# Moving the matmul operands of a decoder layer within their partitions, by padding

## The chip, the cores and the metric

The kernel runs on one core of a Trainium2 chip. The metric is the time of one execution on the device in microseconds, the median of several runs. One execution was also recorded by the hardware profiler; the rows below are from that one.

## What is computed

One layer of a decoder, for 512 tokens of 1024 features, all in float32. Cut to what matters here:

```python
def reference(x, p, ...):
    h = x
    h = h + 0.5 * rms_norm(swiglu(rms_norm(h, ffn1_pre_g), w_gate, w_up, w_down), ffn1_post_g)
    u = rms_norm(h, mix_pre_g)
    proj = u @ w_in                       # queries, keys, forget gates, merge gates, ...
    y_a = dsa_branch(...)                 # attention over keys that an indexer selects
    y_b = ...                             # gated linear recurrence, normed and gated
    merged = sigmoid(gate_a + b) * (y_a @ w_br_a) + sigmoid(gate_b + b) * (y_b @ w_br_b)
    h = h + rms_norm(merged @ w_out, mix_post_g)
    h = h + 0.5 * rms_norm(swiglu(rms_norm(h, ffn2_pre_g), w_gate, w_up, w_down), ffn2_post_g)
    ple_gate = sigmoid(rms_norm(h, ple_pre_g) @ w_ple_gate)
    return h + rms_norm(ple_gate * (p @ w_ple_proj), ple_post_g)

def swiglu(x, w_gate, w_up, w_down):
    return (silu(x @ w_gate) * (x @ w_up)) @ w_down       # 1024 -> 2816 -> 1024
```

## The kernel before

Activations lie with features on the 128 partitions and the 512 tokens along a partition. Every large product is made in three float32r matmuls: both operands are split into a high part, rounded to float32r, and a low part, the rest; the product is high x high, low weights x high, high weights x low, all added up in one bank of PSUM. `mm3_step` (line 205; all matmuls of this kind go through `matmul`, line 239) makes these three for one block of 128 input features: `w[:, 0]` is the high and `w[:, 1]` the low part of the weights, `hi` and `lo` those of the activations. A tile of weights is 128 x 1024, so one output block of 128 features takes 8 x 3 = 24 matmuls (21 where seven blocks are summed).

The weights are the stationary operand and the activations the moving one, 512 columns at a time, or 256 where a stage works on half of the tokens so that the norm behind it can start early. Each matmul has a weight load of its own. In a few products the two change places: for keys, values and the last gate the activations (`hg_hi`, `hg_lo`) are stationary and the weights moving.

Three pairs of tiles hold activations that feed products:

- `hg_hi`, `hg_lo` (made in `consts`, 8 x 512 elements of 4 bytes in each partition): the norm operands. They hold the scaled input of both feed-forward stages, of the mixers' projections and of the last gate, and for a while the two branches' outputs before they are merged.
- `hid_hi`, `hid_lo` (made in `ffn`, for each feed-forward stage): the hidden activations, operands of the second product, in three groups of 8, 7 and 7 blocks.
- `m_hi`, `m_lo` (made in `merge`): the merged mixers, operands of the product with `w_out`.

A weight comes from memory in one transfer (`raw`, three buffers), ScalarE writes its high part, VectorE or GpSimd its low part, into one of six tiles `w` of 2 x 1024 elements. Tiles are laid one behind the other in a partition in the order in which pools hand them out, so the size of an early tile moves all that follow. `r` (4 elements) and `R` (512) are the inverse norms of the tokens. The mixers' stage runs the projections beside the attention, its indexer and the recurrence in an order written out in a table (`PLAN`). The indexer's products have `kidxT` moving and `st` stationary (`dots`, line 508), the recurrence has float32 products of a tile `hX` with itself (lines 698 to 748).

Where these tiles begin in a partition, in bytes, in the program before: `hg_hi` 18336, `hg_lo` 34720, the six `w` 65440 and then every 8192, `hid_hi` and `m_hi` 164512, `hid_lo` and `m_lo` 180896. All of these are 160 modulo 256, and each block of 128 weights (512 bytes) and of 512 tokens (2048 bytes) begins at a multiple of 256 from its tile's start. `kidxT` is at 160 modulo 256 too; `st` is at 32.

Of the kernel before, what the change touches and what calls it, by code (L numbers as in the profile page):

```python
# [7 lines left out]
F32 = mybir.dt.float32  # L8
F32R = mybir.dt.float32r
# [5 lines left out]
P = 128  # L15
D = 1024
NT = 512
KT = D // P
# [52 lines left out]
class Layer:  # L71
# [27 lines left out]
    def consts(self):  # L99
        nc, c = self.nc, self.const  # L100
        self.ident = c.tile([P, P], F32, name="ident")
        self.vecs = c.tile([P, NVEC], F32, name="vecs")
        nc.sync.dma_start(self.vecs, self.a["vecs"])
        self.ones = c.tile([P, P], F32, name="ones")
        nc.gpsimd.memset(self.ones, 1.0)
        self.mhalf = c.tile([P, 16], F32, name="mhalf")
        nc.gpsimd.memset(self.mhalf, -0.5)
        self.ghalf = {}
        for n in ("ffn1_post", "ffn2_post"):
            t = c.tile([P, KT], F32, name=f"half_{n}")  # L110
            nc.vector.tensor_scalar_mul(t, self.gain(n), 0.5)
            self.ghalf[n] = t
        lb = self.vecs[:, LB:LB + 8].rearrange("p (l h) -> p l h", l=2)
        top = c.tile([P, HG], F32, name="lb_top")
        nc.vector.tensor_tensor(top, lb[:, 0], lb[:, 1], op=OP.max)
        e = c.tile([P, 2, HG], F32, name="lb_e")
        for l in range(2):
            nc.vector.tensor_tensor(e[:, l], lb[:, l], top, op=OP.subtract)
        nc.scalar.activation(e, e, AF.Exp)
        den = c.tile([P, HG], F32, name="lb_den")  # L120
        nc.vector.tensor_tensor(den, e[:, 0], e[:, 1], op=OP.add)
        nc.vector.reciprocal(den, den)
        self.lb = c.tile([P, HG], F32, name="lb")
        nc.vector.tensor_tensor(self.lb, e[:, 0], den, op=OP.mult)
        self.lb1 = c.tile([P, HG], F32, name="lb1")
        nc.vector.tensor_scalar(self.lb1, self.lb, -1.0, 1.0, op0=OP.mult, op1=OP.add)
        self.lbn = c.tile([P, HG], F32, name="lbn")
        nc.vector.tensor_scalar_add(self.lbn, self.lb, -1.0)

        self.r = self.keep.tile([P, 4], F32, name="r")  # L130
        self.hg_hi = self.keep.tile([P, KT, NT], F32R, name="hg_hi")
        self.hg_lo = self.keep.tile([P, KT, NT], F32R, name="hg_lo")
        self.R = self.keep.tile([P, NT], F32, name="R")

    def bias_vector(self):

# [235 lines left out]
    def ffn(self, name, nxt, y, pool, spill=None, begin=None):  # L372
        nc, a = self.nc, self.a
        wg, wu, wd = (a[f"{name}_w_{s}"] for s in ("gate", "up", "down"))
        post = self.ghalf[f"{name}_post"]
        hid_hi = pool.tile([P, 8, NT], F32R, name="hid_hi")
        hid_lo = pool.tile([P, 8, NT], F32R, name="hid_lo")
        acc = self.accum(NT)
        for f0, nf in GROUPS:
            first, last = f0 == 0, f0 + nf == FT  # L380
            j0 = 0
            if first and not begin:
                j0 = 2
                w = [self.first_weights(name, (wg[j], wu[j]), D) for j in range(j0)]
                for cols, tags in zip(HALF, (("mm", "mm", "pl", "pl"), ("pt", "po", "mm", "mm"))):
                    ps = [[self.bank(t)[:, :256] for t in tags[2 * j:2 * j + 2]] for j in range(j0)]
                    self.mm3s([(ps[j][i], w[j][i]) for j in range(j0) for i in range(2)], self.hg_hi, self.hg_lo, KT, cols)
                    for j in range(j0):
                        self.hidden(hid_hi, hid_lo, j, *ps[j], cols)
            elif first:  # L390
                j0 = 1
                w = begin[0](wg[0], wu[0])
                ps = self.bank("pl"), self.bank("pt")
                self.mm3s(list(zip(ps, w)), self.hg_hi, self.hg_lo, KT, FULL)
                begin[1]()
                self.hidden(hid_hi, hid_lo, 0, *ps, FULL)
            for j in range(j0, nf):
                pg, pu = self.bank(), self.bank()
                self.mm3(pg, self.weight(wg[f0 + j], D), self.hg_hi, self.hg_lo, KT, FULL)
                self.mm3(pu, self.weight(wu[f0 + j], D), self.hg_hi, self.hg_lo, KT, FULL)  # L400
                self.hidden(hid_hi, hid_lo, j, pg, pu, FULL)
            w = {}

            def product(m, cols):
                if m not in w:
                    w[m] = self.weight(wd[m][:, f0 * P:(f0 + nf) * P], nf * P)
                n = cols.stop - cols.start
                ps = self.bank()[:, :n]
                self.mm3(ps, w[m], hid_hi, hid_lo, nf, cols)
                if first:  # L410
                    nc.scalar.copy(y[:, m, cols], ps)
                else:
                    nc.vector.tensor_tensor(y[:, m, cols], y[:, m, cols], ps, op=OP.add)
                if last:
                    self.square_sum(acc[:, cols], y[:, m, cols], m == 0, nc.vector if m == KT - 1 else nc.gpsimd)

            if last:
                self.last_product(product, y, acc, post, nxt, TURN[name], spill)
                if begin:
                    self.ple_proj(pool)  # L420
            elif first and begin:
                for m in range(KT):
                    product(m, FULL)
                begin[2]()
            else:
                for m in range(KT):
                    product(m, FULL)
# [453 lines left out]
    def merge(self, pool):  # L881

        nc, a = self.nc, self.a
        y = pool.tile([P, KT, NT], F32, name="y_mix")
        m_hi = pool.tile([P, KT, NT], F32R, name="m_hi")
        m_lo = pool.tile([P, KT, NT], F32R, name="m_lo")
        w, first = {}, {}

        def branch(m, b):
            t = pool.tile([P, NT], F32, tag=f"g{b}", name=f"g{b}", bufs=LEAD + 2 if b == 0 else 2)  # L890
            j = b * KT + m
            nc.sync.dma_start(t, self.gate_d[j])
            nc.vector.tensor_tensor(t, t, self.R, op=OP.mult)
            nc.scalar.activation(t, t, AF.Sigmoid, bias=self.vecs[:, GATE_B + j:GATE_B + j + 1])
            if b == 0:
                w[m] = self.weight(a["w_br"][m], D)
            ps = self.bank()
            self.mm3(ps, w[m], self.hg_hi[:, 4 * b:4 * b + 4, :], self.hg_lo[:, 4 * b:4 * b + 4, :], 4, FULL, b * 512)
            nc.vector.tensor_tensor(t, t, ps, op=OP.mult)
            return t  # L900


        for i in range(KT + LEAD):
            if i < KT:
                first[i] = branch(i, 0)
            m = i - LEAD
            if m >= 0:
                t = branch(m, 1)
                nc.gpsimd.tensor_tensor(t, t, first[m], op=OP.add)
                self.split(m_hi[:, m, :], m_lo[:, m, :], t)  # L910
        for k in range(KT):
            nc.sync.dma_start(self.h[:, k, :], self.h_d[k])
        acc = self.accum(NT)
        w = {}

        def product(m, cols):
            if m not in w:
                w[m] = self.weight(a["w_out"][m], D)
            n = cols.stop - cols.start
            ps = self.bank()[:, :n]  # L920
            self.mm3(ps, w[m], m_hi, m_lo, KT, cols)
            nc.scalar.copy(y[:, m, cols], ps)
            self.square_sum(acc[:, cols], ps, m == 0, nc.vector if m == KT - 1 else nc.gpsimd)

        self.last_product(product, y, acc, self.gain("mix_post"), "ffn2_pre", TURN["mix"])
# [175 lines left out]
```

## Time and profile before

| | |
|---|---|
| median of three runs | 1253.28 us (1251.13 to 1253.41) |
| the profiled execution | 1254.52 us |
| its span, first to last instruction | 1252.7 us |
| TensorE busy | 1228.4 us, 6263 matmuls |
| VectorE busy | 706.7 us |
| ScalarE busy | 530.3 us |
| GpSimd busy | 297.8 us |
| moved from and to memory | 131.29 MB, mean 105 GB/s |

The profile's page gives the busy time of each engine over the span, and then groups of instructions by the line that issued them. A name like `mm<-hg_hi,w` says that a matmul wrote a PSUM tile of the tag mm and read hg_hi and w. The five tags mm, pl, pt, po and hg are the kinds of PSUM banks; a product goes to whichever is next in a ring. Matmuls are pipelined: one lasts longer than the distance to the start of the next, so the busy time of a group counts overlapping matmuls once, and the mean duration behind it is that of one.

### The profile page before, as it was taken

The numbers are of one execution on the slowest core, as the hardware profiler recorded it, in microseconds if no ns is written. First come the engines' busy times: TensorE is split into PE (matmuls) and PEld (weight loads), VectorE is DVE, ScalarE is ACT, GpSimd is POOL, SyncE is SP. The second block draws the span as 40 slices with busy tenths as digits, with TensorE's granted clock in tenths as the row PEclk, the third lists the DMA queues.
The fourth block names the chain that finished last, engine by engine and source line by source line (L and its number), as shares of the span: only waits on it lengthen the run. The fifth ranks groups of instructions, "written<-read, shape, count | busy, mean of one in ns | idle before, by whom it ended". The sixth has DMA issues, their size and how long they took to land.

```text
span 1252.7 us, 16616 instructions
## 1 busy us (share of the span) xinstructions
PE 1228.4 (98%) x6263; PEld 1031.5 (82%) x6263; DVE 706.7 (56%) x1252; ACT 530.3 (42%) x905; POOL 297.8 (24%) x348
## 2 busy tenths in 40 slices
PE   7999999999999999999999999999999999999997
PEld 5888888888898887888888877888888888888986
DVE  7543226444448659997677558295532444444386
ACT  6423213222336455565767554364332222222363
POOL 3000000000045203636857622360000000000374
PEclk9999999999999999999999999999999999999999
DMA  6433354333245402423221245223333333332141
GB/s 222 135 91 96 88 107 132 111 101 93 78 130 176 140 18 85 128 91 123 68 72 65 97 138 199 76 85 101 112 91 101 99 86 102 101 95 90 52 152 68
DMA packets 45576, 131.29 MB, mean 105 GB/s; under 512 B 5144, under 2 KB 10424, under 8 KB 45496
## 3 DMA queue, kind: packets, MB, share of 16 engines
q1 hardware_dynamic: 45496, 130.24, 33.3%
q8 instruction: 49, 0.80, 0.3%
q14 instruction: 31, 0.25, 0.1%
HBM read 118.16 MB, written 12.06 MB: 104 GB/s over the span
## 4 chain that ended last, share of the span: by engine, by line
PE 82%; DVE 11%; ACT 3%; DMA 2%; issue 1%; SPq 0%; DVEq 0%; POOLq 0%; POOL 0%; ACTq 0%
PE mm L239 33%; PE pl L239 21%; PE po L239 10%; PE pt L239 9%; DVE hg_lo L284 2%; PE po L581 2%; DVE w L165 2%; DVE h L338 1%; DMA g<-gate_d 1%; DVE z L336 1%; PE hg L705 1%; PE pt L577 1%; DVE sc L532 1%; PE pl L560 1%; PE hg L764 1%
## 5 line engine op out<-in xcount | busy, mean ns | idle before, releaser
L163 ACT ACTIVATE w<-raw 128x1024 fp32r<-128x1024 f32 (+5 forms) x205 | 208.5, 1021 | 385.7 <-PE mm L239 111.6
L239 PE MATMUL mm<-hg_hi,w 128*128 128x512 f32 (+1 forms) x1104 | 340.8, 387 | 0.8 <-DVE small L569 0.8
L165 DVE TENSOR_TENSOR w<-raw,w 128x1024 fp32r<-128x1024 f32 (+5 forms) x189 | 227.7, 1208 | 109.8 <-ACT w L163 109.7
L239 PEld LDWEIGHTS mm<-hg_hi,w 128*128 128x128 f32 x1104 | 203.5, 188 | 39.9 <-DVE w L165 1.1
L277 POOL TENSOR_TENSOR acc<-acc,sq 128x256 f32<-128x256 f32 x78 | 68.0, 877 | 683.8 <-ACT sq L276 682.4
L239 PE MATMUL mm<-hg_lo,w 128*128 128x512 f32 (+1 forms) x552 | 212.5, 387 | 1.2 <-DVE hg_lo L284 1.2
L239 PE MATMUL pl<-hg_hi,w 128*128 128x512 f32 (+1 forms) x592 | 174.2, 377 | 5.5 <-ACT w L163 5.2
L239 PEld LDWEIGHTS pl<-hg_hi,w 128*128 128x128 f32 x592 | 108.7, 191 | 25.8 <-ACT w L163 5.2
L239 PEld LDWEIGHTS mm<-hg_lo,w 128*128 128x128 f32 x552 | 103.4, 188 | 21.1 <-DVE hg_lo L284 1.4
L239 PE MATMUL pl<-hg_lo,w 128*128 128x512 f32 (+1 forms) x296 | 110.3, 376 | 0.7 <-DVE hg_lo L284 0.7
L239 PE MATMUL pt<-hg_hi,w 128*128 128x512 f32 (+1 forms) x256 | 79.0, 388 | 0.9 <-ACT w L163 0.6
L239 PE MATMUL pl<-hid_hi,w 128*128 128x512 f32 (+1 forms) x290 | 79.0, 359 | 0.0
L360 DVE TENSOR_TENSOR t<-mm,R 128x512 f32<-128x512 f32 (+1 forms) x44 | 29.1, 663 | 85.9 <-PE mm L239 65.1
L239 PE MATMUL po<-hg_hi,w 128*128 128x512 f32 (+1 forms) x256 | 77.0, 382 | 0.0
L239 PE MATMUL mm<-hid_hi,w 128*128 128x512 f32 (+1 forms) x278 | 75.3, 357 | 0.0
L239 PEld LDWEIGHTS pl<-hg_lo,w 128*128 128x128 f32 x296 | 56.1, 191 | 10.8 <-DVE hg_lo L284 1.0
L239 PEld LDWEIGHTS pl<-hid_hi,w 128*128 128x128 f32 x290 | 51.7, 189 | 8.0
L239 PEld LDWEIGHTS pt<-hg_hi,w 128*128 128x128 f32 x256 | 47.9, 190 | 11.9 <-ACT w L163 1.1
L239 PEld LDWEIGHTS mm<-hid_hi,w 128*128 128x128 f32 x278 | 49.6, 189 | 7.6
L239 PEld LDWEIGHTS po<-hg_hi,w 128*128 128x128 f32 x256 | 47.5, 188 | 9.3
L360 DVE TENSOR_TENSOR t<-pl,R 128x512 f32<-128x512 f32 (+1 forms) x30 | 20.2, 672 | 58.6 <-PE pl L239 58.5
L239 PE MATMUL pl<-hid_lo,w 128*128 128x512 f32 (+1 forms) x145 | 52.0, 359 | 0.0
(300 smaller groups left out, 2132.5 us busy)
## 6 DMA issues: line engine op xcount, KB each, us to landing
raw<-ffn_w_gate SPq DMA_DIRECT2D x43, 512.0 KB, 3.5
raw<-ffn_w_up SPq DMA_DIRECT2D x43, 512.0 KB, 3.6
raw<-ffn_w_down SPq DMA_DIRECT2D x32, 448.0 KB, 3.2
raw<-ffn_w_down SPq DMA_DIRECT2D x16, 512.0 KB, 3.6
raw<-w_gates SPq DMA_DIRECT2D x16, 512.0 KB, 3.5
gate_d<-t SPq DMA_DIRECT2D x16, 256.0 KB, 2.0
raw<-w_br SPq DMA_DIRECT2D x8, 512.0 KB, 3.3
raw<-w_out SPq DMA_DIRECT2D x8, 512.0 KB, 4.2
```

The costliest lines, as they stand in the source:

```text
L163: hi = nc.scalar.activation(w[:, 0, c], raw[:, c], AF.Copy)
L165: lo = eng.tensor_tensor(w[:, 1, c], raw[:, c], w[:, 0, c].bitcast(F32), op=OP.subtract)
L239: i = self.nc.tensor.matmul(*args, **kw)
L277: eng.tensor_tensor(acc[:, c:c + 256], acc[:, c:c + 256], sq, op=OP.add)
L284: lo = nc.vector.scalar_tensor_tensor(self.hg_lo[:, k, cols], self.h[:, k, cols], g, self.hg_hi[:, k, cols].bitcast(F32), op0=OP.mult, op1 ...
L336: nc.vector.scalar_tensor_tensor(z, y[:, k, c], g[:, k:k + 1], bc, op0=OP.mult, op1=OP.mult)
L338: eng.tensor_tensor(self.h[:, k, c], self.h[:, k, c], z, op=OP.add)
L360: self.nc.vector.tensor_tensor(t, ps, self.R[:, cols], op=OP.mult)
L532: nc.vector.match_replace(sc, best, sc, TAKEN)
L560: nc.tensor.matmul(pl, st[:, tok], kh[:, part, :nk], start=(part == 0), stop=(part == 1))
L577: nc.tensor.transpose(pt[:, k], lg[:, k], self.ident)
L581: nc.tensor.matmul(po[rows, tok], self.vh[:, kt, hd * IDX:(hd + 1) * IDX], at[:, kt * P:(kt + 1) * P], start=(kt == 0), stop=(kt == qt))
```

## The change

Pads are put around the tiles, and views cut them off again. `r` grows by 32 elements (128 bytes), which moves `hg_hi` and `hg_lo`; `R` grows by 32 as well, so that all behind it stand where they stood modulo 256. `hid_hi` gets 24 elements (96 bytes) ahead of its data, `hid_lo` 40 behind; `m_hi` gets 40 (160 bytes) ahead and `m_lo` 24 behind. Each pair of pads comes to 256 bytes. No operation is added, and on all five engines the instructions stand in the same order as before.

```diff
-        self.r = self.keep.tile([P, 4], F32, name="r")
+        self.r = self.keep.tile([P, 4 + 32], F32, name="r")[:, :4]
         self.hg_hi = self.keep.tile([P, KT, NT], F32R, name="hg_hi")
         self.hg_lo = self.keep.tile([P, KT, NT], F32R, name="hg_lo")
-        self.R = self.keep.tile([P, NT], F32, name="R")
+        self.R = self.keep.tile([P, NT + 32], F32, name="R")[:, :NT]
...
-        hid_hi = pool.tile([P, 8, NT], F32R, name="hid_hi")
-        hid_lo = pool.tile([P, 8, NT], F32R, name="hid_lo")
+        hid_hi = pool.tile([P, 8 * NT + 24], F32R, name="hid_hi")[:, 24:].rearrange("p (k t) -> p k t", k=8)
+        hid_lo = pool.tile([P, 8 * NT + 40], F32R, name="hid_lo")[:, :8 * NT].rearrange("p (k t) -> p k t", k=8)
...
-        m_hi = pool.tile([P, KT, NT], F32R, name="m_hi")
-        m_lo = pool.tile([P, KT, NT], F32R, name="m_lo")
+        m_hi = pool.tile([P, KT * NT + 40], F32R, name="m_hi")[:, 40:].rearrange("p (k t) -> p k t", k=KT)
+        m_lo = pool.tile([P, KT * NT + 24], F32R, name="m_lo")[:, :KT * NT].rearrange("p (k t) -> p k t", k=KT)
```

The data then begin at these bytes of a partition:

| data | before | modulo 256 | after | modulo 256 | from the weights, modulo 256 |
|---|---|---|---|---|---|
| w (first of six) | 65440 | 160 | 65696 | 160 | 0 |
| hg_hi | 18336 | 160 | 18464 | 32 | 128 |
| hg_lo | 34720 | 160 | 34848 | 32 | 128 |
| hid_hi | 164512 | 160 | 164864 | 0 | 96 |
| hid_lo | 180896 | 160 | 181248 | 0 | 96 |
| m_hi | 164512 | 160 | 164928 | 64 | 160 |
| m_lo | 180896 | 160 | 181312 | 64 | 160 |

The last column is the way from the weights up to the data in the program after; before, all of it is 0.

## Rows read from the trace of the kernel before

**Rows 1.** Page: busy us, share, count by engine; granted clock in 40 slices.

```profile
PE 1228.4 (98%) x6263; PEld 1031.5 (82%) x6263; DVE 706.7 (56%) x1252; ACT 530.3 (42%) x905; POOL 297.8 (24%) x348
...
PEclk9999999999999999999999999999999999999999
```

**Rows 2.** Windows: stretch, its us, busy us (count) by engine, clock, DMA share, GB/s.

```profile
25.00:350.00 325.00, 325.00 (x1437) 268.46 (x1436) 140.34 (x164) 100.17 (x124) 2.79 (x3) 1.00 0.38 108
...
425.00:730.00 305.00, 304.02 (x1655) 250.11 (x1654) 229.33 (x571) 184.03 (x351) 156.27 (x197) 1.00 0.26 84
...
865.00:1165.00 300.00, 300.00 (x1325) 248.42 (x1324) 125.25 (x147) 86.81 (x108) 0.05 (x1) 1.00 0.31 94
```

**Rows 3.** Waits of TensorE, longest in total first: us, times, longest.

```profile
PE pl L239 <- ACT w L163: 5.2, 1, 5.2
PE mm L239 <- DVE hg_lo L284: 3.7, 4, 1.3
PE pt L239 <- DVE hg_lo L284: 1.8, 4, 0.8
```

**Rows 4.** Chain that ended last: start us, us, what, in both feed-forward stages.

```profile
903.48 5.44 PE mm L239 x24
...
359.10 2.52 PE pt L239 x21
```

**Rows 5.** Windows by tile: hg_hi, hg_lo, hid_hi, hid_lo, m_hi, m_lo; TensorE's busy (count) first.

```profile
0.00:1252.70 1252.70, 738.15 (x2480) 454.19 (x2480) 48.70 (x64) 34.52 (x64) 1.00 0.34 105
0.00:1252.70 1252.70, 464.97 (x1240) 232.31 (x1240) 48.70 (x64) 1.00 0.34 105
0.00:1252.70 1252.70, 222.78 (x830) 147.88 (x830) 30.43 (x46) 28.24 (x46) 1.00 0.34 105
0.00:1252.70 1252.70, 147.00 (x415) 78.33 (x415) 30.43 (x46) 1.00 0.34 105
0.00:1252.70 1252.70, 43.97 (x208) 33.70 (x208) 5.45 (x8) 5.02 (x8) 1.00 0.34 105
0.00:1252.70 1252.70, 31.71 (x104) 19.77 (x104) 5.45 (x8) 1.00 0.34 105
```

**Rows 6.** Line 748 alone: count, ns min/median/max, first and last start, forms.

```profile
L748 PE MATMUL hg<-hX x16: 377/379/382, 545.0 to 719.6; 128*128 128x256 f32 x16
```

**Rows 7.** Groups, shapes apart, 900 to 1100 us: count, busy us, mean ns, idle before.

```profile
L239 PE MATMUL mm<-hg_hi,w 128*128 128x512 f32 x128 | 39.4, 389 | 0.0
...
L239 PE MATMUL mm<-hid_hi,w 128*128 128x512 f32 x76 | 23.4, 389 | 0.0
```

**Rows 8.** Groups, shapes apart, 365 to 368 us.

```profile
L239 PE MATMUL mm<-hid_hi,w 128*128 128x256 f32 x9 | 1.7, 283 | 0.0
```

**Rows 9.** The indexer's products (kidxT moving): count, ns min/median/max, first and last start.

```profile
L508 PE MATMUL pl<-kidxT,st x16: 274/282/288, 428.0 to 465.9; 128*128 128x256 f32 x16
L508 PE MATMUL po<-kidxT,st x16: 389/394/402, 436.0 to 470.7; 128*128 128x512 f32 x16
L508 PE MATMUL pt<-kidxT,st x16: 337/344/346, 436.5 to 469.8; 128*128 128x384 f32 x16
```

**Rows 10.** Groups, shapes apart, of the mixers, 425 to 730 us.

```profile
L239 PE MATMUL mm<-hg_hi,w 128*128 128x512 f32 x526 | 170.4, 397 | 0.8 <-DVE small L569 0.8
L239 PE MATMUL mm<-hg_lo,w 128*128 128x512 f32 x264 | 104.7, 397 | 0.0
```

**Rows 11.** Timeline of TensorE, 441 to 445 us: start us, us, instruction.

```profile
442.23 0.62 PE L508 MATMUL po<-kidxT,st 128*128 128x512 f32 x2
442.69 0.40 PE L624 MATMUL mm<-w,hg_hi 128*128 128x512 f32 x1
442.93 0.39 PE L625 MATMUL mm<-w,hg_lo 128*128 128x512 f32 x1
443.15 0.40 PE L623 MATMUL mm<-w,hg_hi 128*128 128x512 f32 x1
443.39 0.39 PE L624 MATMUL mm<-w,hg_hi 128*128 128x512 f32 x1
```

## The prediction

> **What bounds the kernel now.** I read the first section of the page, then the busy time by stage, then the chain of work that ended last, and last the groups that keep shapes apart. TensorE is busy 1228.4 of 1252.7 us and its granted clock is nine tenths of full speed, 2.4 GHz, or more in every slice [rows 1]. In the two feed-forward stages it is busy for all of 325 and all of 300 us, in the mixers for 304 of 305, while VectorE and ScalarE stay under half in the feed-forward stages and VectorE reaches three quarters in the mixers [rows 2]. TensorE's longest wait is 5.2 us, once, and the thirteen other rows of its waits come to 13.0 us [rows 3]. So the time is the number of matmuls times the spacing from one start to the next, and nothing that the change does to other engines can show before that spacing changes.
>
> The spacing is read from the chain: 24 matmuls of 512 columns take 5.44 us, that is 226.7 ns each, and 21 of 256 columns take 2.52 us, 120.0 ns each [rows 4]. At 2.4 GHz 512 columns are 213.3 ns and 256 are 106.7 ns, so each matmul pays 13.3 ns on top of its columns, whatever its length. The duration that a row gives for one matmul is the spacing plus about 162 ns (389 for 512 columns, 283 for 256) [rows 7, 8], so a difference of durations is a difference of spacings. Each matmul has a weight load of 128 columns of its own, one load in the trace for each matmul [rows 1]; it lies beside the matmul before it.
>
> **The change part by part.** No instruction is added, removed or moved: the built programs have the same rows in the same order on all five engines. What moves is where six tiles of operands lie in a partition. Taken modulo 256, the weights stay at 160, the norm operands go from 160 to 32, the second products' operands from 160 to 0 and the merged mixers' from 160 to 64. Padding costs no time by itself: it is memory that no instruction reads or writes. ScalarE's and VectorE's writes of these tiles move with them; should one of them cost a tenth more, it would lie beside a TensorE that is full (in the last feed-forward stage VectorE has 175 of 300 us free, ScalarE 213) [rows 2], so I cost it at nothing. If that cover were gone, 64 writes of hg_lo at 48.7 us in all [rows 5] would give 5 us at most.
>
> What remains is one term: how many matmuls read a moved tile, times what their spacing changes. The counts, matmuls that read hg_hi, hg_lo, hid_hi, hid_lo, m_hi and m_lo, are 2480 + 1240 + 830 + 415 + 208 + 104 = 5277 of 6263 [rows 1, 5].
>
> The price of one has no row of its own, since in the kernel before every such pair lies at distance 0. I bound it by the nearest rows.
> - The lower end is 10 ns less. The 256-column float32 product of the recurrence lasts 379 ns, with extremes of 377 and 382, where 256 columns in float32r last 283 [rows 6, 8]: by its spacing of about 217 ns it takes two array cycles a column, so 512 cycles, as many as a 512-column float32r matmul, which lasts 389 [rows 7]. It has a weight load of 128 columns too and its two operands also lie at distance 0, both in hX. What differs is that its moving operand is read half as fast. So 10 of the 13.3 ns belong not to loading weights as such but to reading the moving operand at full rate beside the load, which is what a collision of the two reads would look like.
> - The upper end is 6 ns more. The indexer's products read kidxT at 160 with stationary st at 32, the distance of 128 that the norm operands get. They take 394 ns at the median for 512 columns, 5 over the steady 389, and 344 for 384 columns where 389 less 128 columns (53.3 ns) would be 335.7 [rows 7, 9]. The same rows for 256 columns run from 274 to 288 around the steady 283 [rows 8, 9]: 9 less to 5 more, at one and the same distance. They come in pairs between other work, so they show the start of a new pattern and not its steady state.
>
> So the distance does matter to a matmul, and the sign at rest is not in the trace. Rows that lie off the steady pattern are worth a look as well: in the mixers the matmuls on hg_hi and hg_lo, all at distance 0, average 397 ns instead of 389 [rows 7, 10], and behind an indexer pair the starts are 0.22 to 0.24 us apart, 0.70 us for three where the steady three take 0.68 [rows 4, 11]. The steady 226.7 ns is thus a pattern into which the two reads fall, not a floor.
>
> I take 6 ns less. It is nearest to the float32 row, which is the only steady one, and short of it because a weight load of 512 bytes goes round 256 bytes twice while the moving operand passes 256 bytes every 64 columns: two reads that both wander cannot stay apart for a whole load from any start. The sum: 5277 x 6 ns = 31.7 us. TensorE's waits do not eat it: with 2.5% less time per product the weights must come 2.5% faster, and the DMA engines are busy 31 to 38% of the feed-forward stages [rows 2]. The profiled execution took 1254.5 us, 1.8 around its span of 1252.7; less 31.7 it is 1222.8. Its time is 1.2 over the median of 1253.28, so against the median I say 1222.
>
> One rule of the Trainium skill speaks against all this. The rows show that a matmul's spacing is not fixed by its shape (274 to 288 ns for one shape) [rows 9]. "SBUF — State Buffer", section "Who interferes with whom", gives TensorE two read ports, one for the moving operand and one for the weights, and says that TensorE never waits on anyone; by that rule an address would change nothing. It is the second rival below.
>
> "TensorE: Matmul & The Clock Gate", section "Wait — 56ns, not 53.3ns?", gives columns over 2.4 GHz plus about 2.5 ns as the spacing of warm matmuls; an estimate by that page would take 10.9 ns off each, 57 us in all. No 512-column matmul in the steady stages of this trace comes near it.
>
> **The rivals.**
> - *Slower: the steady pattern is lost and none as good is found.* At distance 0 both reads start in the same place and the trace shows that they lock at 226.7 ns. At 128 the pairs that are seen cost 5 to 8 ns more [rows 9]. For: those rows, and 397 in the mixers, where other work breaks the lock [rows 10]. Against: the 274 among the same rows, and that they are starts. Price: 5 ns on the 3720 matmuls on hg_hi and hg_lo alone is 18.6 us, giving 1272; on all 5277 it is 26.4, giving 1280. It decides where the average of the three distances comes out above 226.7 ns; I give it 0.34, since it is the only case for which the trace shows the very distance.
> - *No change.* This decides if the 13.3 ns, the same for 256 and 512 columns [rows 4], are a fixed cost of swapping weights, and addresses have no part in it: 1253. Against: 379 ns for a product that swaps weights too [rows 6]. That the pads do not do what they say is part of this case, but the built addresses are those of the diff's words. 0.13.
> - *Faster by the whole collision.* All 10 ns go: 52.8 us, giving 1200. This is the end of the forecast's own range. 0.08 for this or below.
>
> **How the numbers follow.** Faster with some but not all of the collision gone: 0.45, its own range 1200 to 1245; with the last rival's 0.08 the chance of faster is 0.53. Same 0.13, slower 0.34. Cases of both signs hold most of the chance, so the range must reach across: from 1200 (0.08 below) to 1277, which takes in the slower case up to 4.5 ns on all matmuls and leaves about 0.11 above. A difference of about 0.2%, 2.5 us, is what a measurement of this kernel can tell from none; the three chances are for that bound.
>
> **What would show it.** In the chain of the changed kernel, 24 matmuls of the last feed-forward stage should take 5.3 us instead of 5.44, and the rows of mm<-hg_hi should fall from 389 to about 383 ns; mm<-hid_hi and m_hi have distances of their own, so each may do something else, and the three rows apart tell which of the pads earns or costs. If the slower rival holds, the same rows read 394 or more, and their minimum and maximum spread as in the mixers. If rows stay at 389 and 283, addresses play no part. The forecast would be wrong if the 10 ns of the float32 row come from the slower column rate itself and not from the reads. It would also be wrong if the faster products meet a wait for weights, which would be seen as idle time before TensorE, released by ScalarE or VectorE at the weights' split.

## The result: slower by 1.6%

The changed kernel takes 1273.24 us (median of four runs, 1272.53 to 1273.80), the kernel before 1253.17 in the same comparison (1251.13 to 1253.41). The ratio is 1.016 with a 95% interval of 1.0147 to 1.0173. The profiled execution took 1273.80 us and its span is 1272.0, so the span grew by 19.3 us. The forecast of 1222 us was wrong in sign; the time is inside the range, and it is that of the rival "the steady pattern is lost" (1272).

The first section of the page, of the changed kernel (busy us, share, count; granted clock in 40 slices), beside [rows 1]:

```profile
PE 1250.4 (98%) x6263; PEld 1033.8 (81%) x6263; DVE 707.3 (56%) x1252; ACT 530.8 (42%) x905; POOL 298.2 (23%) x348
...
PEclk9999999999999999999999999999999999999999
```

All counts are those of before, and so are the busy times of VectorE, ScalarE and GpSimd, to 0.6 us. TensorE alone is busy longer: 22.0 us. Its granted clock is nine tenths or more in every slice, as before.

Windows by stage, beside [rows 2] (stretch, its us, busy us and count by engine, clock, DMA share, GB/s):

```profile
25.00:350.00 325.00, 325.00 (x1400) 261.84 (x1399) 134.53 (x158) 94.48 (x117) 1.02 (x2) 1.00 0.37 105
425.00:730.00 305.00, 304.61 (x1636) 248.77 (x1635) 231.58 (x572) 183.51 (x344) 154.44 (x195) 1.00 0.27 87
865.00:1165.00 300.00, 300.00 (x1292) 242.36 (x1291) 124.07 (x148) 85.07 (x107) 0.00 (x0) 1.00 0.31 95
```

TensorE is as full as before, and in the same stretches it gets through fewer matmuls: 1437, 1655 and 1325 have become 1400, 1636 and 1292. That is 2.6% more time for one in the feed-forward stages and 1.4% in the mixers. Its waits have not grown (us in total, times, longest; beside [rows 3]):

```profile
PE pl L239 <- ACT w L163: 5.1, 1, 5.1
PE mm L239 <- DVE hg_lo L284: 3.1, 3, 1.3
PE pt L239 <- DVE hg_lo L284: 1.8, 4, 0.8
```

The chain that ended last gives the new spacing (start us, us, what). The first row is 21 matmuls of 256 columns of the first stage's second product, the next 24 of 512 columns of a second product in the last stage (hid, distance 96), the last one 24 of a first product behind it (hg, distance 128):

```profile
363.43 2.52 PE mm L239 x21
...
971.23 5.60 PE mm L239 x24
976.83 5.58 PE pl L239 x24
```

5.60 us is 233.3 ns each and 5.58 is 232.5, against 226.7 [rows 4]. The 256 columns still take 2.52 us. The groups of the last stage, shapes apart (count, busy us, mean ns), beside [rows 7], read

```profile
L239 PE MATMUL mm<-hg_hi,w 128*128 128x512 f32 x114 | 35.7, 394 | 0.0
...
L239 PE MATMUL mm<-hid_hi,w 128*128 128x512 f32 x76 | 23.8, 394 | 0.0
```

and those of the mixers, beside [rows 10],

```profile
L239 PE MATMUL mm<-hg_hi,w 128*128 128x512 f32 x537 | 175.2, 400 | 0.4 <-DVE small L569 0.4
L239 PE MATMUL mm<-hg_lo,w 128*128 128x512 f32 x268 | 107.1, 400 | 0.0
```

So 389 has become 394, and 397 has become 400. How far single ones spread in the last stage (line, count, ns min/median/max, first and last start):

```profile
L239 PE MATMUL mm<-hid_hi,w x15: 392/392/394, 971.1 to 976.0; 128*128 128x512 f32 x15
L239 PE MATMUL mm<-hg_hi,w x51: 390/393/404, 1004.5 to 1049.9; 128*128 128x512 f32 x51
```

The starts, read one by one, show that this is not scatter: in the last stage the steps of hg go round in seven (228, 230, 233, 241, 232, 231, 232 ns, each to within one, mean 232.4), those of hid in three (231, 231, 238, mean 233.3). In the kernel before, every step of the steady stretches is 226.7 ns. So it is again a steady pattern, only a longer one.

**Where the 19.3 us are.** I added up, in both traces, the distance from each matmul's start to the next one's, by operand and columns, waits included:

| moving operand | columns | matmuls in the trace | before, us | after, us | difference |
|---|---|---|---|---|---|
| hg | 512 | 3024 | 701.9 | 717.5 | +15.6 |
| hid | 512 | 867 | 196.6 | 202.4 | +5.8 |
| hid | 256 | 378 | 45.6 | 45.7 | 0.0 |
| m | 512 | 72 | 19.1 | 18.1 | -1.0 |
| m | 256 | 240 | 28.9 | 28.4 | -0.5 |
| hg | 256 | 288 | 43.7 | 41.6 | -2.1 |
| w (hg stationary) | 200 | 96 | 11.4 | 13.3 | +1.9 |

They come to 19.7 us. The rows of m with 512 columns, hg with 256 and w with 200 hold waits at the edges of stages; their differences are partly that. Two rows carry the result, and both are 512-column products with a moved tile as the moving operand.

### The profile page after: what moved, and what is told of

Its sections match the earlier page's. It is cut to its first block, busy times and chain, and to the rows that moved or that the text cites. A ratio compares the mean times of both kernels' runs of the same rounds, so it can differ in the third digit from the quotient of the medians.

```text
span 1272.0 us, 16616 instructions
## 1 busy us (share of the span) xinstructions
PE 1250.4 (98%) x6263; PEld 1033.8 (81%) x6263; DVE 707.3 (56%) x1252; ACT 530.8 (42%) x905; POOL 298.2 (23%) x348
## 4 chain that ended last, share of the span: by engine, by line
PE 86%; DVE 8%; ACT 2%; DMA 2%; issue 1%; SPq 0%; DVEq 0%; POOLq 0%; POOL 0%; ACTq 0%
PE mm L239 36%; PE pl L239 21%; PE po L239 10%; PE pt L239 10%; DVE hg_lo L284 2%; PE po L581 2%; PE hg L705 1%; DVE h L338 1%; DVE z L336 1%; DMA g<-gate_d 1%; DVE w L165 1%; PE pt L577 1%; PE pl L560 1%; PE hg L764 1%; PE mm L623 1%
## 5 line engine op out<-in xcount | busy, mean ns | idle before, releaser
L239 PE MATMUL mm<-hg_hi,w 128*128 128x512 f32 (+1 forms) x1104 | 345.5, 391 | 0.4 <-DVE small L569 0.4
L239 PEld LDWEIGHTS mm<-hg_hi,w 128*128 128x128 f32 x1104 | 203.8, 188 | 43.7 <-DVE w L165 0.7
```

What stands on the lines that cost most here:

```text
L239: i = self.nc.tensor.matmul(*args, **kw)
```

## The experiments

Each diff is against the kernel before. The first four and the kernel before were timed in rounds together (before: 1253.15 us); the others are single runs beside one run of before (1253.81 us, and 1253.38 for the third and fourth of the other distances and for the two runs on the moving read), where a difference of 2.5 us means little and the rows say more.

**One pad at a time.** Which of the three moves costs?

```diff
-        self.r = self.keep.tile([P, 4], F32, name="r")
+        self.r = self.keep.tile([P, 4 + 32], F32, name="r")[:, :4]
...
-        self.R = self.keep.tile([P, NT], F32, name="R")
+        self.R = self.keep.tile([P, NT + 32], F32, name="R")[:, :NT]
```

> Only the norm operands are moved, 128 bytes from the weights modulo 256. Distance theory (what counts is how far a moving operand lies from the weights): the groups on hg_hi and hg_lo rise from 389 to about 394 ns as in the changed kernel, those on hid_hi and hid_lo stay at 389, time about 1267 us (+14). Rival, a side effect of the pads on the writers or on what lies behind: no such split between the groups, and a time that does not follow the count of matmuls on hg_hi and hg_lo.

Measured: 1267.23 us, ratio 1.0107 (1.0088 to 1.0125), so +14. In its chain the second product keeps 5.44 us for 24 matmuls and the first product behind it takes 5.60:

```profile
968.86 5.44 PE mm L239 x24
...
985.49 5.60 PE pl L239 x24
```

The second products' pads alone:

```diff
-        hid_hi = pool.tile([P, 8, NT], F32R, name="hid_hi")
-        hid_lo = pool.tile([P, 8, NT], F32R, name="hid_lo")
+        hid_hi = pool.tile([P, 8 * NT + 24], F32R, name="hid_hi")[:, 24:].rearrange("p (k t) -> p k t", k=8)
+        hid_lo = pool.tile([P, 8 * NT + 40], F32R, name="hid_lo")[:, :8 * NT].rearrange("p (k t) -> p k t", k=8)
```

> Only the second products' operands are moved, 96 bytes. Distance theory: 867 matmuls of 512 columns go from 226.7 to 233.3 ns, +5.8 us, the 378 of 256 columns stay at 120 on average: about 1259 us; the groups on hg_hi stay at 389. Rival, the norm operands alone carry the loss: 1253 us.

Measured: 1260.32 us, ratio 1.0055 (1.0040 to 1.0070), +7. Now the chain changes the other way round, second product first:

```profile
955.74 5.60 PE po L239 x24
...
983.30 5.44 PE pt L239 x24
```

The merged mixers' pads alone:

```diff
-        m_hi = pool.tile([P, KT, NT], F32R, name="m_hi")
-        m_lo = pool.tile([P, KT, NT], F32R, name="m_lo")
+        m_hi = pool.tile([P, KT * NT + 40], F32R, name="m_hi")[:, 40:].rearrange("p (k t) -> p k t", k=KT)
+        m_lo = pool.tile([P, KT * NT + 24], F32R, name="m_lo")[:, :KT * NT].rearrange("p (k t) -> p k t", k=KT)
```

> Only the merged mixers' operands are moved, 160 bytes. Distance theory: 72 matmuls of 512 columns lose 6 ns each and 240 of 256 columns gain 2 ns each, which cancel: 1253 us, no difference that can be measured. Rival, a distance of 160 is good and only 128 and 96 are bad: 1 us less or more cannot be told in the time, but the 512-column groups on m_hi would not lengthen.

Measured: 1253.02 us, ratio 0.9995 (0.9985 to 1.0004), no difference. Its groups, shapes apart (count, busy us, mean ns):

```profile
L239 PE MATMUL mm<-m_hi,w 128*128 128x256 f32 x48 | 8.8, 282 | 0.0
...
L239 PE MATMUL mm<-m_hi,w 128*128 128x512 f32 x16 | 5.2, 397 | 0.0
```

In the kernel before these two groups read

```profile
L239 PE MATMUL mm<-m_hi,w 128*128 128x256 f32 x48 | 8.9, 285 | 0.0
...
L239 PE MATMUL mm<-m_hi,w 128*128 128x512 f32 x16 | 5.1, 391 | 0.0
```

At distance 160 the short ones gain about 3 ns and the long ones lose 6, and there are 240 of the first to 72 of the second. The three pads add up: 14 + 7 + 0 against the 20 of the whole change.

**All moved together.** Is it the place of a tile or its distance from the weights? Only `r` is padded, so that norm operands, weights, second products' operands and merged mixers all move by 128 bytes, to 32 modulo 256, and the distance is 0 again.

```diff
-        self.r = self.keep.tile([P, 4], F32, name="r")
+        self.r = self.keep.tile([P, 4 + 32], F32, name="r")[:, :4]
```

> The pad behind r stays, the one behind R goes, so norm operands, weights, second products' operands and merged mixers all move 128 bytes together: their places modulo 256 are new (32), their distances are 0 as before. Distance theory: steady groups back at 389 ns, about 1253 us. Rival, the operand's own place in the 256 bytes counts (160 is good, 32 is not): groups at 394 or more and 1273 us or longer.

Measured: 1252.71 us, ratio 0.9997 (0.9987 to 1.0006). Groups of its last stage:

```profile
L239 PE MATMUL mm<-hg_hi,w 128*128 128x512 f32 x128 | 39.4, 389 | 0.0
...
L239 PE MATMUL mm<-hid_hi,w 128*128 128x512 f32 x76 | 23.4, 389 | 0.0
```

All is as before: of these two places, 160 and 32, neither is the better, and it is the distance that counts. Writes by ScalarE and VectorE moved here as well and cost nothing.

**Other distances.** Is 0 a good distance or only not the worst? Four kernels differ from the changed one in the pads' sizes alone; their diffs show the new lines. The first gives hg 64, hid 128 and m 32 bytes:

```diff
+        self.r = self.keep.tile([P, 4 + 16], F32, name="r")[:, :4]
+        self.R = self.keep.tile([P, NT + 48], F32, name="R")[:, :NT]
+        hid_hi = pool.tile([P, 8 * NT + 32], F32R, name="hid_hi")[:, 32:].rearrange("p (k t) -> p k t", k=8)
+        hid_lo = pool.tile([P, 8 * NT + 32], F32R, name="hid_lo")[:, :8 * NT].rearrange("p (k t) -> p k t", k=8)
+        m_hi = pool.tile([P, KT * NT + 8], F32R, name="m_hi")[:, 8:].rearrange("p (k t) -> p k t", k=KT)
+        m_lo = pool.tile([P, KT * NT + 56], F32R, name="m_lo")[:, :KT * NT].rearrange("p (k t) -> p k t", k=KT)
```

> Other distances, one for each kind of operand: norm operands 64 bytes, second products' operands 128, merged mixers 32. Theory that distance 0 alone gives a steady pattern at rest: groups on hg_hi near 394 ns (1267 us for them alone), groups on hid_hi at 128 bytes near 394 like hg_hi at 128 in the changed kernel (it is the distance that counts and not the tile), together about 1273 us. Rival, that two reads 64 bytes apart keep out of each other's way: hg_hi below 389.

Measured: 1261.71 us. hid first, then hg, in the chain:

```profile
956.73 5.57 PE po L239 x24
...
984.37 5.49 PE pt L239 x24
```

64 bytes cost 228.8 ns (5.49 us for 24), the mildest of all that were moved, and less than was expected of it. The second kernel of this kind gives hg 192, hid 224 and m 192:

```diff
+        self.r = self.keep.tile([P, 4 + 48], F32, name="r")[:, :4]
+        self.R = self.keep.tile([P, NT + 16], F32, name="R")[:, :NT]
+        hid_hi = pool.tile([P, 8 * NT + 56], F32R, name="hid_hi")[:, 56:].rearrange("p (k t) -> p k t", k=8)
...
+        m_hi = pool.tile([P, KT * NT + 48], F32R, name="m_hi")[:, 48:].rearrange("p (k t) -> p k t", k=KT)
...
```

> Norm operands 192 bytes, second products' operands 224, merged mixers 192. Theory that distance 0 alone gives a steady pattern: hg_hi and hid_hi near 394 to 396, about 1273 us. Rival, a distance below 0 (192 is -64, 224 is -32) is better than one above, since the weights are then read ahead of the moving operand: 383 to 389 and 1225 to 1253 us.

Measured: 1272.25 us; hid and hg both 5.60 us for 24:

```profile
958.51 5.60 PE pt L239 x24
...
980.91 5.60 PE mm L239 x24
```

The rival, that a distance below 0 is better than one above, falls with it. The third has hg 32, hid 192 and m 64 (`r` + 8, `R` + 56, `hid_hi` + 48, `m_hi` + 16 elements, and the rest of 64 behind):

```diff
+        self.r = self.keep.tile([P, 4 + 8], F32, name="r")[:, :4]
...
+        hid_hi = pool.tile([P, 8 * NT + 48], F32R, name="hid_hi")[:, 48:].rearrange("p (k t) -> p k t", k=8)
...
```

> Norm operands 32 bytes, second products' operands 192, merged mixers 64. Theory that only at distance 0 a matmul of 512 columns settles at 226.7 ns: hg_hi between 391 (what 64 bytes gave) and 395, hid_hi near 395 as norm operands at 192, m_hi's 256-column matmuls below 283 as at every other distance. Rival, a small distance is as good as none: hg_hi at 389.

Measured: 1273.04 us. From its chain, hg at 32 in the last stage, and hid at 192 with 256 columns in the first:

```profile
982.33 5.60 PE mm L239 x24
...
365.72 2.47 PE pl L239 x21
```

At 32 bytes hg is as slow as at 192: a small distance is not as good as none. The fourth has hg 224, hid 64 and m 96 (`r` + 56, `hid_hi` + 16, `m_hi` + 24):

```diff
+        self.r = self.keep.tile([P, 4 + 56], F32, name="r")[:, :4]
...
+        hid_hi = pool.tile([P, 8 * NT + 16], F32R, name="hid_hi")[:, 16:].rearrange("p (k t) -> p k t", k=8)
...
```

> Norm operands 224 bytes, second products' operands 64, merged mixers 96. Same theory: hg_hi near 395 as the second products' operands at 224, hid_hi near 391 as norm operands at 64; about 1268 us. Rival, the tile counts and not the distance: the values of the two tiles at one distance differ by more than 2 ns.

Measured: 1271.63 us. From its chain, all of hid at 64: 21 matmuls of 512 columns in the second group of blocks of the first stage, 21 of 512 and 21 of 256 in the third, and in the last stage 24 of 512:

```profile
259.95 4.90 PE pl L239 x21
...
357.67 4.81 PE pl L239 x21
...
364.86 2.38 PE pl L239 x21
...
959.45 5.60 PE pt L239 x24
```

The same distance thus gives 229.0 ns in one group of blocks (4.81 us for 21) and 233.3 in another of the same stage, in the same tiles (4.90). The first group has 5.49 us for 24 in the first stage and 5.60 in the last. The distance does not settle the pattern alone. The pads on hg alone show this too: its rows read 5.57 to 5.59 us in the first stage and 5.60 in the last. From the chains of all these kernels:

| distance, bytes | 512 columns, ns | read from | 256 columns (hid), ns |
|---|---|---|---|
| 0 | 226.7 | hg, hid | 120.0 |
| 32 | 233.3 | hg | |
| 64 | 228.8 to 233.3 | hg, hid | 113.3 to 118.1 |
| 96 | 233.3 | hid | 120.0 |
| 128 | 232.1 to 233.3 | hg, hid | 118.1 to 119.0 |
| 192 | 233.3 | hg, hid | 113.3 to 118.6 |
| 224 | 233.3 | hg, hid | 118.1 to 118.6 |

For 512 columns 0 is the best and every other one in steps of 32 (160 seen only in a few of m) is worse, by 2 to 7 ns. For 256 columns 0 is the worst, beside 96. Where a cell is empty no chain piece of hid shows it; the merged mixers' products of 256 columns read 116.7 ns at 32 (2.80 us for 24) and 117.1 to 117.5 at 160.

That the distance counts modulo 256 rests on the kernel before: by the addresses hg lies a multiple of 512 bytes from its weights there and hid an odd multiple of 256, and both read 226.7 ns, while a distance of 128 reads 232.1 to 233.3.

**A load that stays in one place.** The forecast's reason was that the weight load's read wanders into the moving operand's. If the load reads one address only, its read can no longer wander. The gate products take 128 times the same column of weights:

```diff
+    def mm3_gate(self, ps, w, hi, lo, n, cols):
+        for k in range(n):
+            c = slice(k * P, k * P + 1)
+            wh, wl = (w[:, i, c].to_broadcast([P, P]) for i in range(2))
...
-                self.mm3(pg, self.weight(wg[f0 + j], D), self.hg_hi, self.hg_lo, KT, FULL)
+                self.mm3_gate(pg, self.weight(wg[f0 + j], D), self.hg_hi, self.hg_lo, KT, FULL)
```

> Kernel before, but the gate products of both feed-forward stages (those that one group of the loop makes) load a single column of the weights 128 times over, so the load reads one place of a partition and the gates are not the reference's. Collision theory of the prediction (10 of the 13.3 ns come from the load's read beside the moving one): these matmuls fall from 389 towards 379 ns while the up products stay at 389; 20 gate blocks x 24 matmuls x 2 stages x 10 ns is 10 us less. Rival, 226.7 ns is the best that a matmul of this kind has with any load: they stay at 389 and the time at 1253 us.

Measured: 1256.54 us. Chain, an up product and a gate product, and the durations of the gate products that read hg_hi:

```profile
969.38 5.44 PE mm L248 x24
974.82 5.55 PE pl L248 x24
```

```profile
L248 PE MATMUL pl<-hg_hi,w x35: 396/396/397, 979.7 to 1029.8; 128*128 128x512 f32 x35
```

Neither what the collision theory asks for (the fall to 379) nor its rival (389, no effect) came: the gate products go up to 231.3 ns in the mean (two steps of three are 234 ns, the third 226). At distance 0 a load that walks along with the moving operand is cheaper than one that stands still. The same with the pads on `r` and `R`, distance 128 in the place of 0:

```diff
-        self.r = self.keep.tile([P, 4], F32, name="r")
+        self.r = self.keep.tile([P, 4 + 32], F32, name="r")[:, :4]
...
-                self.mm3(pg, self.weight(wg[f0 + j], D), self.hg_hi, self.hg_lo, KT, FULL)
+                self.mm3_gate(pg, self.weight(wg[f0 + j], D), self.hg_hi, self.hg_lo, KT, FULL)
```

> The same single-column loads for the gate products with the norm operands at a distance of 128 bytes. Theory that the added 5 ns come from the load's read meeting the moving one: gate products fall back to 389 or lower, up products stay near 394, time about 1262 us. Rival, they come from the moving operand's own place relative to the matmul before it and not from the load: both stay at 394 and the time at 1267 us.

Measured: 1267.84 us. Gate and up product in the chain:

```profile
972.91 5.55 PE pl L248 x24
978.46 5.58 PE mm L248 x24
```

A load in one place costs the gate products 231.3 ns at either distance; the up products are as slow as the distance makes them. So here too neither of the two expected outcomes came.

**The moving read.** Are the 10 ns of the float32 row in the moving operand's read? First with two-byte operands: the gate products, again by a `mm3_gate` called in place of `mm3`, multiply constant bfloat16 tiles, with a weight load of 128 columns each as before.

```diff
+    def mm3_gate(self, ps, w, hi, lo, n, cols):
+        for k in range(n):
+            x, v = self.xb[:, k % 2, :], self.wb[:, k * P:(k + 1) * P]
...
+        self.xb = pool.tile([P, 2, NT], mybir.dt.bfloat16, name="xb")
+        self.wb = pool.tile([P, D], mybir.dt.bfloat16, name="wb")
+        nc.gpsimd.memset(self.xb, 0.01)
+        nc.gpsimd.memset(self.wb, 0.01)
...
```

> Kernel before, but the gate products of both feed-forward stages multiply constant bfloat16 tiles (so the gates are not the reference's): loads and moving operands have 2 bytes an element, 512 columns as before. Theory that the 13.3 ns come from moving 4 bytes a column at full rate: these matmuls fall to 379 ns or below (216 ns apart), 20 x 24 x 2 x 10 ns is 10 us less, about 1243 us. Rival, they are a fixed cost of a matmul with a new load: 389 and 1253 us.

Measured: 1249.15 us. Gate and up product in the chain of the last stage:

```profile
960.76 5.20 PE pl L247 x24
965.96 5.46 PE mm L247 x24
```

The weight loads of the gate products on its page, and one of its waits (us in total, times, longest):

```profile
L247 PEld LDWEIGHTS <-wb 128*128 128x128 bf16 x984 | 93.4, 98 | 120.7 <-issue 12.7
...
PE hg L269 <- POOL small L238: 2.7, 1, 2.7
```

The gate products fall to 216.7 ns (5.20 us for 24), 10 less; read start by start inside a block it is 215.8. Of the 9.8 us that 984 such products (41 blocks of 24; the blocks that open a stage are made by other lines and stay as they were) would bring at 10 ns each, 4.2 arrived. The up products give back 0.02 us for each 24 at the change of type. More went at the start of the last stage: ahead of it this kernel led by 3.3 us (24 matmuls of the merged mixers' product begin at 790.91 us, in the kernel before at 794.22), and at one of that stage's first full products (864.83 against 863.59) it was 1.2 behind. The row above, a wait of TensorE for GpSimd that the kernel before does not have, lies there. What delays that stretch was not followed up; the gate products are not in it, and the two fills of the constant tiles by GpSimd (0.95 us each) begin only after that wait, at 842.90 us. As the weight loads shrink as well, to 98 ns from 188, this run does not tell which of the two reads the 10 ns belong to.

Then with the types unchanged and the moving operand in one place, one token's column 512 times:

```diff
+    def mm3_gate(self, ps, w, hi, lo, n, cols):
+        for k in range(n):
+            c = slice(k * P, (k + 1) * P)
+            xh, xl = (x[:, k, 0:1].to_broadcast([P, NT]) for x in (hi, lo))
+            self.matmul(ps, w[:, 0, c], xh, start=(k == 0), stop=False)
...
```

> Kernel before, but the gate products of both feed-forward stages read one token's column 512 times over as moving operand (so the gates are not the reference's); loads as before. Theory that the moving operand's walk through the partition meets the load's walk: without the walk these matmuls leave 389, for 379 if the walk is what costs, or for 393 to 396 as with one-column loads, if the walk in step with the load's is what holds the pattern at 389. Rival, the moving operand's addresses have no part in it: 389.

Measured: 1243.82 us, 9.6 less than before, which is nearly all of the 9.8 that 10 ns on 984 products make. Chain and group:

```profile
955.88 5.20 PE pl L248 x24
961.08 5.45 PE mm L248 x24
```

```profile
L248 PE MATMUL pl<-hg_hi,w 128*128 128x512 f32 x128 | 38.2, 380 | 0.0
```

So the 10 ns hang on the moving operand's read along the partition. With that read held in one place they are gone, while the load walks as ever; with the load held in one place they are not. That the four bytes of an element are part of it is only suggested by the run before, where both operands had two.

## Why the prediction was wrong

- **What bounds the kernel: right.** TensorE's spacing is all. Counts, clock, waits and the other engines are unchanged, and the three pads add up, 14 + 7 + 0 us for a total of 20.
- **Padding and the writes at nothing: right.** With everything at 32 modulo 256 the kernel takes 1252.71 us.
- **One price for 5277 matmuls: wrong in the count.** The 906 products of 256 columns on the moved tiles did not get slower (hid 0.0, m -0.5, hg -2.1 us). The 512-column ones of hg and hid, 3891 of them in the table, carry the loss. In the mixers, where the pattern was already broken in the kernel before [rows 10], there was less to lose: 400 ns after 397, against 394 after 389.
- **Six ns less: the step that failed.** It came out as 5.2 ns more on hg (15.6 us over 3024) and 6.7 more on hid (5.8 over 867). I took the value nearest to the float32 row because that was the only steady one [rows 6, 7]; but its 16 products come four at a time, hardly steadier than the indexer's pairs. The 10 ns are real and hang on the moving read, as I said; the run with one token shows it. The false link was the next one: that this was a collision with the weight load which another distance avoids. The load held in one place made it worse, and of the seven distances in the table 0 already costs a 512-column product least. Whether the 10 ns that are left at distance 0 are a collision that no distance avoids, or the price of the walking read alone, is not shown: in every run each matmul has a load beside it.
- **The bound that I set aside had the right number; that it had it for the right reason is not shown.** The indexer's pairs [rows 9] lie at the very distance of the norm operands and read 394 at the median. I held it against them that they only show starts. In the changed kernel the steady hg products read 393 at the median and 394 in the mean. But no run moved kidxT against st, and in the same stage products at distance 0 read 397 [rows 10]. The indexer's rows themselves, whose distance the change leaves alone, do not hold still either: 512 columns read on, and 384 columns, whose 344 I had read as 8 ns lost, fall to 337.

```profile
L508 PE MATMUL po<-kidxT,st x16: 392/395/401, 445.4 to 480.4; 128*128 128x512 f32 x16
L508 PE MATMUL pt<-kidxT,st x16: 334/337/346, 445.9 to 479.5; 128*128 128x384 f32 x16
```

- **The slower rival: right that the steady pattern is lost and none as good is found, its 1272 partly by luck.** What holds the pattern at distance 0 is not shown. It priced 5 ns on 3720 products, 18.6 us. In truth hg's 512-column products lost 15.6 and the second products 5.8, which it had left out. Its other sign held as well: the rows read 394, and minimum and maximum spread from 390 to 404. They spread in a fixed round of seven steps and not, as I wrote, as in the mixers, where other work breaks the pattern.
- **No change: fallen.** The trace shows that addresses alone move the spacing from 226.7 to 233.3 ns. The Trainium skill, "SBUF — State Buffer", section "Who interferes with whom", has TensorE never wait on anyone; by these runs its matmuls do slow down by where their two operands lie. The 2.5 ns that the Trainium skill, "TensorE: Matmul & The Clock Gate", section "Wait — 56ns, not 53.3ns?", adds to the columns' time hold here for two-byte operands (215.8 ns from start to start, an estimate by that page 215.8) and not for float32r that walks (226.7 at best).

**What stays open.** What in the chip makes the rounds of steps was not settled. The lengths of the rounds, though not the single steps in them, are whole multiples of 6.67 ns (226.7 ns is 34 of them, 120.0 is 18, the round of three 105, the round of seven 244), which the runs show but do not explain. Why 64 bytes are milder, and why one distance has two patterns in different groups of blocks, is open too. So is whether a matmul's distance to its own weights counts or to those that are loaded beside it, since all weights lie alike modulo 256. No version with the same results and better than the kernel before was found: moving only the third group of hidden activations by 64 bytes would save 378 products of 256 columns 5.1 ns each (1.9 us) and cost each of 147 of 512 about 2.2 ns (0.3 us), by the spacings of that group in the run at 64, so 1.6 us in all, an estimate and less than a measurement of this kernel can tell. It was not tried.

## What to carry to other kernels

Where TensorE is full and the spacing of its matmuls is an exact, repeating number, that number can be a state which the operands' addresses hold up, as here; a pad put in for any other reason can lose it, so look at the spacing in the chain after every change of layout. For float32r products of 512 columns, each with its own weight load, keep the moving operand and the weights at the same address modulo 256 within a partition. A price read from a row that differs from the case in several things (here the type, the columns and the rate of the read) can be wrong in its sign; a run that moves one tile alone, like the first of these experiments, settles it.

## What the runs showed of the hardware that was not expected

- The spacing of 512-column float32r matmuls depends on the distance of their two operands modulo 256: 226.7 ns at 0, 228.8 to 233.3 at the others tried, at an unchanged granted clock and with no longer waits for other engines. Moving all tiles together by 128 bytes changes nothing (1252.71 us).
- With 256 columns it is the other way: 120.0 ns at 0, down to 113.3 at 64 and 192.
- Off distance 0 most matmuls run in fixed rounds of unequal steps: three or seven in the changed kernel; at 192 bytes the steps of hg are all 233.3 ns. At 128 hg has two rounds, of seven steps (mean 232.4 ns) and, in the last stage of the kernel with the pads on hg alone, of two (229 and 237, mean 233.3).
- A weight load from a single address makes the matmuls slower (231.3 ns) than one that walks through 512 bytes (226.7); a moving operand from a single address makes them faster (216.7), as do two-byte operands (215.8), whose loads also take 98 ns and not 188.
